# A projection kernel with context tokens: weights of the modulation in fours, context products merged, bias loads on another queue

## The chip, the cores and the metric

The kernel runs on one core of a Trainium2 chip. The metric is the device time of one execution in microseconds; a time stands for the median of several executions. TensorE (PE in the profile, with its weight loads as PEld) multiplies matrices, VectorE (DVE) and ScalarE (ACT) work element by element, GpSimd (POOL) does a little of that and issues DMAs, SyncE (SP) only issues DMAs. Each engine runs its own instructions in order, and waits for others through semaphores.

## The reference

One layer: an adaLN-modulated input goes through one wide projection; half of its columns feed a gated position-mixing MLP, the other half a bidirectional state-space scan; both come back through one output projection and a layer norm. Context tokens go through a part of the projection only. What the change touches is the beginning of it:

```python
D_MODEL, SEQ, CTX_LEN = 2048, 1024, 256; W_A = W_B = 1024
mod_x = jax.nn.silu(c) @ w_ada + b_ada                  # (1, 6144)
mod_c = (jax.nn.silu(c_ctx) @ w_ada + b_ada)[None]
shift_x, scale_x, gate_x = jnp.split(mod_x, 3, axis=-1)
shift_c, scale_c, gate_c = jnp.split(mod_c, 3, axis=-1)
proj_x = _modulate(x, shift_x, scale_x) @ w_in          # (1024, 5 * 1024)
hc = _modulate(ctx, shift_c, scale_c)                   # LN(ctx) * (1 + scale) + shift
ub_c = hc @ w_in[:, col_b0:col_b1]                      # (256, 1024)
...
mixed = einsum("hpq,bnqhd->bnphd", w_s, LN(v) * ln_g + ln_b) + b_s   # position mixing
ya_x = u * mixed * silu(za_x)
```

Everything is fp32.

## The kernel before

**Arithmetic.** Each operand of a main product is split in two: `hi` is the value rounded to the short fp32r format (ScalarE, `whi` for weights), `lo` what is left (VectorE, `wlo`). A product then is three: hi·hi, hi·lo, lo·hi (`kstep`, L825 to L829), all summed in one PSUM bank. Every instruction on an engine but the DMAs goes through one wrapper, so the trace gives all of them line L519, and they are told apart by the names of their tiles.

**Weights.** `w_in` comes in chunks of 128x1024 (512 KB), two to a block of 128 output columns: chunk c of a block holds the rows k = 8c to 8c+7 (of 16) of 128 each. `Weights` (L554 to L583) loads a chunk on SP's queue (`wraw`, every third one of the context pass `craw`, L565) and splits it; `wget` (L658) takes chunk i, issues the load of i+2 and then the split of i+1. `wraw`, `whi` and `wlo` have two buffers each, so a load waits for the split of an earlier chunk, and a split for TensorE to be done with an earlier one. Chunks 0 to 7 belong to the blocks v0 to v3, 8 and 9 to `zb` 0, 10 to 25 to the eight context blocks `cx` (chunk 11 is the second half of the first one).

**Prologue (L735 to L954).** `x` is normalised, transposed and modulated in 32 units (k, h) (k: 128 of the 2048 input columns; h: half of the rows), and each unit at once goes through three main products blocks (`pro_main`, b = 0, 1, 2). The shift and scale that unit k needs come from `matvec` (L767): `w_ada` comes in 64 segments `ada` of 512 KB, eight for each group s of 256 columns of `x`; a segment i is two fp32 products, into the quarters `q = i % 2 * 2 + j` (j = 0, 1) of the 128 output partitions of a `sy` bank. After the eighth, ScalarE copies the bank to `mvs` and `mods` (L784) sums its quarters by transposes and a VectorE reduction into `ss`. The loads: 16 segments lie in slots, 3 in `wpool`, the rest in a ring of five; when segment n is done, the load of n+5 is issued (`ada_load`, L748). The main loop runs over the 32 units; four steps (j = 0 to 3) belong to one group s = 2 to 7, and `cut` says which segments are taken after which step: `cut = 0, 3, 5, 7`, that is three after j = 0, two after j = 1, two after j = 2, and the last at the beginning of the step j = 3.

**Context pass (L1003 to L1103).** `ctx_task` makes the context tile `cT` (128 x 16 x 2 x 256: 16 k, hi and lo, 256 tokens), interleaved with the blocks v3 and zb0. Then `zb_out` evicts zb0 through SiLU (`szb`) and stores it on ScalarE's queue (`tmp_sz`). `bias_task` (L1043) loads `ws` and `bs` (512 KB each, in pieces of 512 B) on SP's queue, multiplies ones by `ws` (two `sy` products) and adds to `bs` on VectorE; its `bs` takes the buffer of `szb` (tag `stb`), so the load waits for that store. The loop over eight blocks m and 16 k makes three products of 256 columns for each k into `e[:, :256]`; ScalarE copies the block to `usc`, GpSimd's queue stores it (`tmp_ubc`):

```python
kstep([(e[:, :256], cxT)], wt, 8 * c + kk, c + kk == 0, c == 1 and kk == 7)
```

The interleaving of the tasks is decided while the program is built, by modelled clocks (`until`, `room`, `pump`), not on the chip.

Of the kernel before, what the change touches and what calls it, by code (L numbers as in the profile page):

```python
# [9 lines left out]
FT = mybir.dt.float32  # L10
FR = mybir.dt.float32r
I32 = mybir.dt.int32
AF = mybir.ActivationFunctionType
# [11 lines left out]
def dap(t, offset, ap):  # L25
    return bass.AP(tensor=t.tensor, offset=t.offset + offset, ap=[list(a) for a in ap])
# [559 lines left out]
def build(tc, a, out, scratch):  # L586
    nc = Metered(tc.nc)
    ck = nc.clock
    V, S, T, P, SP = nc.vector, nc.scalar, nc.tensor, nc.gpsimd, nc.sync
# [13 lines left out]
    def bank(tag, bufs):  # L603
        return (sb[1] if tag == "sb" else pp).tile([128, 512], FT, name=tag, tag=tag, bufs=bufs)

    def slot(dt, name, h):

        return slots.tile([128, 1024], dt, name=name, tag=f"slot{h}", bufs=16)

    def parts(name, h):  # L610
        t = slot(FR, name, h)
        return t[:, 0:512], t[:, 512:1024]


    chunks, first = [], {}
# [23 lines left out]
    W = Weights(nc, wpool, chunks)  # L639
# [18 lines left out]
    def wget(key, held=0):  # L658

        i = first[key]  # L660
        r = W.get(i)
        W.load_to(i + 2 - held)
        if not held:
            W.split_to(i + 1)
        return r
# [4 lines left out]
    def pump(n=1):  # L670
        for _ in range(n):
            for t in list(tasks):
                if next(t, StopIteration) is StopIteration:
                    tasks.remove(t)

    def wait(n):
        for _ in range(n):
            yield

    def until(t):  # L680

        while ck.pe < t:
            yield
# [11 lines left out]
    def drain(*ts):  # L695

        while any(t in tasks for t in ts) if ts else tasks:
            ck.pe += 1300
            pump()
# [13 lines left out]
    sc = consts.tile([128, 2, 16], FT, name="sc")  # L713
# [22 lines left out]
    pro_p = pro.enter_context(tc.tile_pool(name="pro", bufs=1))  # L736
# [4 lines left out]
    ada = {j: slot(FT, "ada", j // 8).rearrange("p (j c) -> p j c", j=2) for j in range(16)}  # L741
    xn = [[slot(FT, "xn", h).rearrange("p (t c) -> p t c", t=4) for h in range(2)] for _ in range(8)]

    def x_in(h, s0, s1):
        for s in range(s0, s1):
            SP.dma_start(xn[s][h], dap(a["x"], h * 512 * D + s * 256, [[D, 128], [128 * D, 4], [1, 256]]))

    def ada_load(j):  # L748
        if j < 64:
            if 15 < j < 19:  # L750
                ada[j] = wpool.tile([128, 2, 512], FT, name="ada", tag=("whi", "wlo", "wlo")[j - 16])
            elif j > 18:
                ada[j] = pro_p.tile([128, 2, 512], FT, name="ada", bufs=5)
            SP.dma_start(ada[j], a["w_mod"][j // 8, j // 2 % 4][:, j % 2 * 2:j % 2 * 2 + 2])

    def norm(s, h, ts=range(4)):
# [8 lines left out]
    mvb = {}  # L765

    def matvec(s, i0, i1):  # L767

        for i in range(i0, i1):
            if i == 0:  # L770
                mvb[s] = bank("sy", 1)
            n = 8 * s + i
            t = ada.pop(n)
            for j in range(2):
                q = i % 2 * 2 + j
                T.matmul(mvb[s][32 * q:32 * q + 32], cs[:, 2 * i + j], t[:, j], start=(i < 2), stop=(i > 5),
                         skip_group_check=True)
            if n > 18:
                ada_load(n + 5)
            if i == 7:  # L780
                mvs = mvb[s, 1] = pro_p.tile([128, 512], FT, name="mvs")
                S.activation(mvs, mvb[s], AF.Copy)

    def mods(s):  # L784
# [30 lines left out]
    def modulate(n):  # L815

        k, h = units[n]
        sh, sl = ss[:, k // 2, k % 2, 0:1], ss[:, k // 2, 2 + k % 2, 0:1]
        xm = pro_p.tile([128, 512], FT, name="xm")
        S.activation(xm, tp.pop(n), AF.Identity, bias=sh, scale=sl)  # L820
        hi, lo = xT[h][k] = parts("xT", h)
        S.activation(hi, xm, AF.Copy)
        V.tensor_sub(lo, xm, hi.bitcast(FT))

    def kstep(banks, wt, k, st, en):  # L825
        for p_, (i, j) in enumerate(((0, 0), (0, 1), (1, 0))):
            for o, x in banks:
                T.matmul(o, wt[i], x[k][j], start=st and p_ == 0, stop=en and p_ == 2,
                         skip_group_check=True)  # L829

    def block(key, order=(0, 1)):
        o = [bank("mm", 4) for _ in range(2)]
        n = 0
        for c in order:
            hi, lo = wget((key, c))
            for kk in range(8):
                k = 8 * c + kk
                wt = (hi[:, kk * 128:kk * 128 + 128], lo[:, kk * 128:kk * 128 + 128])
                kstep(list(zip(o, xT)), wt, k, n == 0, n == 15)
                n += 1  # L840
                pump()
        return o
# [5 lines left out]
    def pro_main(k, h, b):  # L848
# [3 lines left out]
        hi, lo = wt0[b, c]  # L852
        wt = (hi[:, kk * 128:kk * 128 + 128], lo[:, kk * 128:kk * 128 + 128])
        kstep([(vb[b][h], xT[h])], wt, k, k == 0, k == 15)
    cut = 0, 3, 5, 7
    units = [(k, h) for h in range(2) for k in range(2)] + [(k, h) for k in range(2, 16) for h in range(2)]

    def early(s):
# [19 lines left out]
    x_stats(0, 0, 8)  # L878
    ln_finish(0, 4)
    x_in(1, 0, 8)  # L880
    for j in range(8, 24):
        ada_load(j)
    w3_load(1)
    for s in range(8):
# [11 lines left out]
    for i, (k, h) in enumerate(units):  # L896
        s, j = divmod(i + 5, 4)
# [61 lines left out]
    def v_out(m, o):  # L959
        vg = st_p.tile([128, 1024], FT, name="vg", tag="sta")  # L960
        for h in range(2):
            S.activation(vg[:, halves[h]], o[h], AF.Gelu)
        vt = st_p.tile([128, 8, 128], FT, name="vt", tag="stb")
        yield from wait(2)
        for h in range(2):
            pt = bank(("ps", "sy")[h], 1)
            for i in range(4):
                T.transpose(pt[:, i * 128:i * 128 + 128], vg[:, (4 * h + i) * 128:(4 * h + i) * 128 + 128], ident)
            yield
            S.activation(vt[:, 4 * h:4 * h + 4].rearrange("p a b -> p (a b)"), pt, AF.Copy)  # L970
            for i in range(4):
                V.bn_stats(stats[:, 4 * h + i, m], vt[:, 4 * h + i])
            yield
        S.dma_start(scratch["v"][m], vt)

    def v_first():
        for b in (0, 2, 1):
            yield from v_out(b, vb[b])
        while len(vb) < 4:
            yield  # L980
        yield from v_out(3, vb[3])
    vf = v_first()
    next(vf)
    tasks.append(vf)

    def zb_out(m, o):
        zs = st_p.tile([128, 1024], FT, name="szb", tag="stb")
        for c in range(2):
            S.activation(zs[:, halves[c]], o[c], AF.Silu)
        S.dma_start(scratch["sz"][m], zs)  # L990
# [4 lines left out]
    cT = cT_p.tile([128, 16, 2, 256], FR, name="cT")  # L995
    cxT = {k: (cT[:, k, 0], cT[:, k, 1]) for k in range(16)}
# [38 lines left out]
    vb.append(o)  # L1035
    o = block(("zb", 0))
    drain()
    zb_out(0, o)

    cl_es.close()  # L1040
# [2 lines left out]
    def bias_task():  # L1043

        ws = st_p.tile([128, 8, 128], FT, name="ws", tag="sta")
        SP.dma_start(ws, dap(a["w_sp"], 0, [[128, 128], [16384, 8], [1, 128]]))
        bs = st_p.tile([128, 8, 128], FT, name="bs", tag="stb")
        SP.dma_start(bs, dap(a["b_sp"], 0, [[0, 128], [128, 8], [1, 128]]))
        yield from until(ck.pe + 20000)
        for h0 in (0, 4):  # L1050
            rs = bank("sy", 1)
            T.matmul(rs, ones, ws[:, h0:h0 + 4].rearrange("p h d -> p (h d)"), start=True, stop=True)
            yield from wait(2)
            for h in range(h0, h0 + 4):
                V.scalar_tensor_tensor(bs[:, h], rs[:, 128 * (h - h0):128 * (h - h0) + 128], vecs[:, 1, h:h + 1],
                                       bs[:, h], op0=OP.mult, op1=OP.add)
            yield from until(ck.pe + 4000)
        S.dma_start(dap(scratch["bp"], 0, [[128, 128], [16384, 8], [1, 128]]), bs)
# [34 lines left out]
    for m in range(8):  # L1093
        e = bank("sb", 2)
        for c in range(2):
            hi, lo = wget((("cx", m), c))
            for kk in range(8):
                wt = (hi[:, kk * 128:kk * 128 + 128], lo[:, kk * 128:kk * 128 + 128])
                kstep([(e[:, :256], cxT)], wt, 8 * c + kk, c + kk == 0, c == 1 and kk == 7)
                pump()  # L1100
        us = us_p.tile([128, 8, KC], FT, name="usc")
        S.activation(us[:, ::-1].rearrange("p j k -> p k j"), e[:, :256].rearrange("p (k j) -> p k j", j=8), AF.Copy)
        P.dma_start(dap(scratch["ubc"], m * 128 * 8 * KC, [[8 * KC, 128], [1, 8 * KC]]), us.rearrange("p j k -> p (j k)"))  # L1103
    drain()
    us_es.close()
# [126 lines left out]
    for m in range(8):  # L1232
        o = block(("ub", m))
        us = s2.tile([128, 8, KL], FT, name="us", tag="vh")
# [114 lines left out]
    for m in range(8):  # L1349
# [8 lines left out]
        for k in range(8):  # L1358
            wt = (hi[:, k * 128:k * 128 + 128], lo[:, k * 128:k * 128 + 128])
# [147 lines left out]
    for t in range(4, 8):  # L1507
# [7 lines left out]
        for i, x, y in ((0, 0, 1024), (1, 0, 1024)) if t < 7 else ((0, 0, 1024), (1, 0, 512), (1, 512, 1024)):  # L1515
            z, c = z1[t - 4, i][:, x:y], slice(1024 * i + x, 1024 * i + y)
# [60 lines left out]
```

## Times and profile before

| | us |
|---|---|
| median of 3 runs | 1620.19 |
| lowest, highest | 1620.13, 1622.97 |
| profiled execution | 1618.88 |
| its span (first to last instruction) | 1616.8 |
| PE busy | 1571.3 |
| DVE busy | 1071.4 |
| ACT busy | 504.5 |

The profile's times count from the start of the span of that one execution. An engine's busy time says how much of the span it worked, not whether the end waited for it; that is read from the chain of waits, which follows the work that ended last back from one releaser to the one before, and from the idle time that a row of the timeline shows in brackets ahead of an instruction, with what ended it. Beside them, PEclk is the TensorE clock that was granted, as a share of full speed (1.00 is 2.4 GHz, 0.50 is 1.2 GHz).

### The profile page before, as it was taken

The numbers are of one execution on the slowest core, as the hardware profiler recorded it, in microseconds if no ns is written. First come the engines' busy times: TensorE is split into PE (matmuls) and PEld (weight loads), VectorE is DVE, ScalarE is ACT, GpSimd is POOL, SyncE is SP. The second block draws the span as 40 slices with busy tenths as digits, with TensorE's granted clock in tenths as the row PEclk, the third lists the DMA queues.
The fourth block names the chain that finished last, engine by engine and source line by source line (L and its number), as shares of the span: only waits on it lengthen the run. The fifth ranks groups of instructions, "written<-read, shape, count | busy, mean of one in ns | idle before, by whom it ended". The sixth has DMA issues, their size and how long they took to land.

```text
span 1616.8 us, 22311 instructions
## 1 busy us (share of the span) xinstructions
PE 1571.3 (97%) x8468; PEld 1269.8 (79%) x8468; DVE 1071.4 (66%) x1960; ACT 504.5 (31%) x831; POOL 184.7 (11%) x286
## 2 busy tenths in 40 slices
PE   4999999999999999999999999999999999999996
PEld 2556889888888888888888888888888888888775
DVE  8542635982988889888888898166565633465557
ACT  2544653112322233233233333211533412133210
POOL 0000000000222222222222222121000000012000
PEclk9999999999999999999999999999999999999998
DMA  9885354334444444444434443477445533365422
GB/s 338 318 321 177 149 170 158 120 123 130 114 120 127 114 128 122 116 128 128 127 99 128 128 116 89 139 249 248 182 146 167 202 132 121 108 239 176 137 85 104
DMA packets 134211, 251.37 MB, mean 155 GB/s; under 512 B 53972, under 2 KB 74580, under 8 KB 132312
## 3 DMA queue, kind: packets, MB, share of 16 engines
q1 hardware_dynamic: 112200, 208.73, 39.9%
q0 software_dynamic: 16384, 31.78, 7.0%
q10 hardware_dynamic: 5520, 9.44, 1.6%
q8 instruction: 66, 1.08, 0.3%
q14 instruction: 41, 0.34, 0.1%
HBM read 213.60 MB, written 36.12 MB: 154 GB/s over the span
## 4 chain that ended last, share of the span: by engine, by line
PE 86%; DVE 5%; DMA 5%; ACT 3%; issue 1%; SPq 1%; ACTq 0%; DVEq 0%
PE mm L519 65%; PE sb L519 9%; PE sy L519 8%; PE ps L519 3%; DMA wraw<-in_w_out_dram 2%; DVE wlo L519 1%; ACT whi L519 1%; DVE stats L519 1%; DVE z L519 1%; DMA wraw<-in_w_in_dram 1%; DVE xn L519 1%; ACT xm L519 1%; DMA xn<-in_x_dram 1%; DMA cl<-in_ctx_dram 0%; DMA ada<-in_w_mod_dram 0%
## 5 line engine op out<-in xcount | busy, mean ns | idle before, releaser
L519 PE MATMUL mm<-xT,whi 128*128 128x512 f32 x2496 | 687.9, 395 | 1.6 <-ACT vg L519 0.7
L519 PEld LDWEIGHTS mm<-xT,whi 128*128 128x128 f32 x2496 | 462.0, 188 | 108.0 <-issue 6.9
L519 PE MATMUL mm<-xT,wlo 128*128 128x512 f32 x1248 | 391.4, 391 | 0.0
L519 DVE TENSOR_TENSOR wlo<-wraw,whi 128x1024 fp32r<-128x1024 f32 (+1 forms) x164 | 200.0, 1222 | 287.3 <-ACT whi L519 287.1
L519 ACT ACTIVATE whi<-wraw 128x1024 fp32r<-128x1024 f32 (+1 forms) x164 | 170.0, 1039 | 407.4 <-PE mm L519 212.5
L519 PEld LDWEIGHTS mm<-xT,wlo 128*128 128x128 f32 x1248 | 234.7, 188 | 50.8 <-DVE wlo L519 0.9
L519 DVE TENSOR_TENSOR p<-sb,ue 128x640 f32<-128x640 f32 x64 | 49.7, 819 | 50.0 <-PE sb L519 49.9
L519 PE MATMUL mm<-whi,yb 128*128 128x512 f32 x256 | 79.9, 389 | 0.0
L519 PE MATMUL mm<-y,whi 128*128 128x512 f32 x256 | 68.4, 389 | 0.0
L519 POOL TENSOR_TENSOR zs<-zs,dsk 128x16 f32<-128x16 f32 x32 | 18.1, 565 | 423.0 <-ACT zs L519 423.0
L519 PE MATMUL sy<-ada,cs 128*32 128x512 f32 x256 | 41.5, 621 | 18.8 <-DMA ada<-in_w_mod_dram 18.8
L519 PE MATMUL mm<-whi,ya 128*128 128x512 f32 x192 | 59.5, 389 | 0.0
L519 POOL TENSOR_TENSOR z<-z,lnb 128x1024 f32<-128x1024 f32 x8 | 19.2, 2396 | 346.0 <-ACT z L519 346.0
L519 PEld LDWEIGHTS mm<-whi,yb 128*128 128x128 f32 x256 | 48.1, 188 | 9.9
L519 PEld LDWEIGHTS mm<-y,whi 128*128 128x128 f32 x256 | 48.0, 188 | 9.9
L519 DVE TENSOR_TENSOR xT<-xm,xT 128x512 fp32r<-128x512 f32 x32 | 22.1, 692 | 49.5 <-ACT xT L519 49.5
L519 PE MATMUL sb<-cT,whi 128*128 128x256 f32 x256 | 48.6, 292 | 2.6 <-ACT whi L519 2.6
L519 PE MATMUL mm<-wlo,yb 128*128 128x512 f32 x128 | 49.9, 390 | 0.0
L519 DVE TENSOR_TENSOR_SCAN p<-ur,p 128x640 f32<-128x640 f32 x32 | 47.7, 1491 | 3.0 <-DVE ut L519 0.5
L519 PE MATMUL sb<-whi,yb 128*128 128x512 f32 x128 | 45.4, 396 | 1.5 <-ACT whi L519 1.5
L403 POOL DMA_DIRECT2D tmp_z<-zs x64 | 44.1, 691 | 11.2 <-POOL zs L519 9.2
L519 DVE TENSOR_TENSOR p<-p,ue 128x512 f32<-128x512 f32 x64 | 44.2, 690 | 1.7
(270 smaller groups left out, 2325.6 us busy)
## 6 DMA issues: line engine op xcount, KB each, us to landing
wraw<-in_w_in_dram SPq DMA_DIRECT2D x89, 512.0 KB
ada<-in_w_mod_dram SPq DMA_DIRECT2D x64, 512.0 KB
wraw<-in_w_out_dram SPq DMA_DIRECT2D x64, 512.0 KB
gw<-in_w_gate_dram POOLq DMA_DIRECT2D x32, 512.0 KB, 6.0
xn<-in_x_dram SPq DMA_DIRECT2D x16, 512.0 KB
upf<-tmp_pf SPq DMA_DIRECT2D x32, 256.0 KB
ubb<-in_b_c_dram SPq DMA_DIRECT2D x32, 256.0 KB
tmp_v<-vt ACTq DMA_DIRECT2D x8, 512.0 KB
```

What stands on the lines that cost most here:

```text
L403: nc.gpsimd.dma_start(dap(d["z5"], (z["g0"] + q) * 32 * 144, [[72, 2], [144, 32], [1, 72]]), zs[64 * q:64 * q + 64])
L519: r = f(*args, **kw)
```

## The change

There are five edits. (1) `cut` becomes `0, 4, 4, 8`: four segments after j = 0, none after j = 1, four after j = 2, none at j = 3; the ring of segments gets a sixth buffer, one more is loaded ahead, and `mvs` and `xm` take one buffer in turn. (2) The split of chunk 11 is issued ahead of the SiLU evictions of zb0. (3) A SiLU on one element, at the end of `v_first`, brings the function table load earlier. (4) `ws` and `bs` are loaded on GpSimd's queue. (5) In the context loop whi·[hi | lo] is one product of 512 columns into the whole bank `e`, and wlo·hi one of 256 into its first half; at the block's end VectorE adds the second half to `usc`.

```diff
-                ada[j] = pro_p.tile([128, 2, 512], FT, name="ada", bufs=5)
+                ada[j] = pro_p.tile([128, 2, 512], FT, name="ada", bufs=6)
...
-                ada_load(n + 5)
+                ada_load(n + 6)
             if i == 7:
-                mvs = mvb[s, 1] = pro_p.tile([128, 512], FT, name="mvs")
+                mvs = mvb[s, 1] = pro_p.tile([128, 512], FT, name="mvs", tag="mvs")
...
-        xm = pro_p.tile([128, 512], FT, name="xm")
+        xm = pro_p.tile([128, 512], FT, name="xm", tag="mvs")
...
-    cut = 0, 3, 5, 7
+    cut = 0, 4, 4, 8
...
-    for j in range(8, 24):
+    for j in range(8, 25):
         ada_load(j)
...
         yield from v_out(3, vb[3])
+        S.activation(sc[:, 1, 0:1], sc[:, 1, 0:1], AF.Silu)
...
     o = block(("zb", 0))
     drain()
+    W.split_to(first[("cx", 0), 1])
     zb_out(0, o)
...
-        SP.dma_start(ws, dap(a["w_sp"], 0, [[128, 128], [16384, 8], [1, 128]]))
+        P.dma_start(ws, dap(a["w_sp"], 0, [[128, 128], [16384, 8], [1, 128]]))
...
-        SP.dma_start(bs, dap(a["b_sp"], 0, [[0, 128], [128, 8], [1, 128]]))
+        P.dma_start(bs, dap(a["b_sp"], 0, [[0, 128], [128, 8], [1, 128]]))
...
-                kstep([(e[:, :256], cxT)], wt, 8 * c + kk, c + kk == 0, c == 1 and kk == 7)
+                k = 8 * c + kk
+                T.matmul(e, wt[0], cT[:, k].rearrange("p i t -> p (i t)"), start=k == 0, stop=False,
+                         skip_group_check=True)
+                T.matmul(e[:, :256], wt[1], cxT[k][0], start=False, stop=k == 15, skip_group_check=True)
                 pump()
...
-        S.activation(us[:, ::-1].rearrange("p j k -> p k j"), e[:, :256].rearrange("p (k j) -> p k j", j=8), AF.Copy)
+        usk = us[:, ::-1].rearrange("p j k -> p k j")
+        S.activation(usk, e[:, :256].rearrange("p (k j) -> p k j", j=8), AF.Copy)
+        V.tensor_add(usk, usk, e[:, 256:].rearrange("p (k j) -> p k j", j=8))
```

In the main loop of the prologue, TensorE's order before, from the end of a step j = 0 (the segments `sy<-ada,cs`; the products of the next unit; a transpose `ps<-io,xn`); a row counts each product once, the trace counts an fp32 one twice:

```order
L519 MATMUL sy<-ada,cs 32x512 x6
L519 MATMUL mm<-xT,whi 128x512 x2
L519 MATMUL mm<-xT,wlo 128x512
L519 MATMUL mm<-xT,whi 128x512 x2
L519 MATMUL mm<-xT,wlo 128x512
L519 MATMUL sb<-xT,whi 128x512 x2
L519 MATMUL sb<-xT,wlo 128x512
L519 MATMUL sy<-ada,cs 32x512 x4
L519 MATMUL ps<-io,xn 128x128 x4
```

The same place after:

```order
L519 MATMUL sy<-ada,cs 32x512 x8
L519 MATMUL mm<-xT,whi 128x512 x2
L519 MATMUL mm<-xT,wlo 128x512
L519 MATMUL mm<-xT,whi 128x512 x2
L519 MATMUL mm<-xT,wlo 128x512
L519 MATMUL sb<-xT,whi 128x512 x2
L519 MATMUL sb<-xT,wlo 128x512
L519 MATMUL ps<-io,xn 128x128 x4
```

The fourth segment joined the first three, and none is left between this step and the transpose of the next.

ScalarE's order before, from the last context tile to the eviction of the first context block:

```order
L519 ACTIVATE xm<-sb,ss 128x128
L519 ACTIVATE cT<-xm 128x128
L519 ACT_TABLE_LOAD
L519 ACTIVATE szb<-mm 128x512 x2
L990 DMA tmp_sz<-szb 128x1024
L519 ACTIVATE whi<-wraw 128x1024 x2
L519 ACTIVATE usc<-sb 128x32x8
```

The same place after:

```order
L519 ACTIVATE xm<-sb,ss 128x128
L519 ACTIVATE cT<-xm 128x128
L519 ACTIVATE whi<-wraw 128x1024
L519 ACTIVATE szb<-mm 128x512 x2
L991 DMA tmp_sz<-szb 128x1024
L519 ACTIVATE whi<-wraw 128x1024
L519 ACTIVATE usc<-sb 128x32x8
```

The first of the two `whi` (chunk 11) went ahead of the `szb` evictions, and the table load is gone from here.

SP's queue before, from the loads of chunks 11 and 12 on:

```order
L565 DMA wraw<-in_w_in_dram 128x1024 x2
L1046 DMA ws<-in_w_sp_dram 128x8x128
L1048 DMA bs<-in_b_sp_dram 128x1024
L565 DMA wraw<-in_w_in_dram 128x1024
L565 DMA craw<-in_w_in_dram 128x1024
L565 DMA wraw<-in_w_in_dram 128x1024 x2
```

The same place after:

```order
L565 DMA wraw<-in_w_in_dram 128x1024 x3
L565 DMA craw<-in_w_in_dram 128x1024
L565 DMA wraw<-in_w_in_dram 128x1024 x2
L565 DMA craw<-in_w_in_dram 128x1024
L565 DMA wraw<-in_w_in_dram 128x1024 x2
```

The load of chunk 13 now follows that of chunk 12 directly; `ws` and `bs` stand on GpSimd's queue ahead of the eight `tmp_ubc` stores.

## Rows read from the trace of the kernel before

**Rows 1.** Page, busy time: engine, us (share of the span), instructions.
```profile
PE 1571.3 (97%) x8468; PEld 1269.8 (79%) x8468; DVE 1071.4 (66%) x1960; ACT 504.5 (31%) x831; POOL 184.7 (11%) x286
```

**Rows 2.** Windows: us, busy PE PEld DVE ACT POOL, PEclk, DMA share, GB/s.
```profile
220.00:240.00 20.00, 19.48 (x149) 19.24 (x148) 6.64 (x7) 7.86 (x9) 1.82 (x3) 0.91 0.69 234
...
300.00:320.00 20.00, 20.00 (x90) 16.57 (x89) 19.15 (x49) 2.93 (x3) 0.53 (x1) 1.00 0.26 101
```

**Rows 3.** Chain of waits in the prologue: start us, us, what.
```profile
50.00 1.85 PE sy L519 x16
...
59.87 1.84 PE sy L519 x12
...
64.01 1.00 PE sy L519 x8
...
92.37 6.58 DMA ada<-in_w_mod_dram
```

**Rows 4.** Timeline of TensorE behind that transfer: start us, us, instruction [idle before].
```profile
98.99 1.05 PE L519 MATMUL sy<-ada,cs 128*32 128x512 f32 x4 [0.23 <-DMA ada<-in_w_mod_dram]
```

**Rows 5.** Window of 4 us in the prologue.
```profile
88.00:92.00 4.00, 4.00 (x22) 1.92 (x21) 2.12 (x5) 2.35 (x5) 0.00 (x0) 1.00 1.03 408
```

**Rows 6.** Timelines of ScalarE, VectorE, TensorE and SP, start of the context pass.
```profile
199.08 1.06 ACT L519 ACTIVATE whi<-wraw 128x1024 fp32r<-128x1024 f32 x1 [1.72 <-PE mm L519]
...
213.79 1.28 ACT L519 ACT_TABLE_LOAD   x1
...
216.58 2.00 ACT L519 ACTIVATE whi<-wraw 128x1024 fp32r<-128x1024 f32 x2 [0.40 <-ACT szb L519]
...
217.66 2.36 DVE L519 TENSOR_TENSOR wlo<-wraw,whi 128x1024 fp32r<-128x1024 f32 x2 [3.56 <-ACT whi L519]
...
212.10 0.40 PE L519 MATMUL sb<-cT,whi 128*128 128x256 f32 x2
...
217.68 0.50 PE L519 MATMUL sb<-cT,whi 128*128 128x256 f32 x2 [2.55 <-ACT whi L519]
...
226.98 0.39 PE L519 MATMUL sb<-cT,wlo 128*128 128x256 f32 x1 [0.52 <-DVE wlo L519]
...
218.88 0.33 SPq L1048 DMA_DIRECT2D bs<-in_b_sp_dram  x1
```

**Rows 7.** Chain of waits, in the context pass and further on.
```profile
219.31 5.22 DMA wraw<-in_w_in_dram
...
239.93 0.86 PE sy L519 x2
...
246.68 19.40 PE sb L519 x162
...
1378.30 43.52 PE mm L519 x192
...
1529.78 3.20 DMA wraw<-in_w_out_dram
```

**Rows 8.** Window of 1 us in the first context block.
```profile
221.00:222.00 1.00, 1.00 (x7) 1.00 (x7) 0.00 (x0) 0.00 (x0) 0.00 (x0) 0.50 0.80 201
```

**Rows 9.** Timelines of VectorE and of the weight loads, end of a context block.
```profile
231.45 1.23 DVE L519 TENSOR_TENSOR wlo<-wraw,whi 128x1024 fp32r<-128x1024 f32 x1 [2.99 <-ACT whi L519]
...
232.73 0.19 PEld L519 LDWEIGHTS sb<-cT,wlo 128*128 128x128 f32 x1
```

**Rows 10.** Timeline of VectorE; page, DMA queues (packets, MB, share) and issues.
```profile
240.83 1.13 DVE L519 SCALAR_TENSOR_TENSOR bs<-sy,vecs,bs 128x128 f32<-128x128 f32 x4
243.79 1.23 DVE L519 TENSOR_TENSOR wlo<-wraw,whi 128x1024 fp32r<-128x1024 f32 x1 [1.83 <-ACT whi L519]
...
288.40 0.43 DVE L519 TENSOR_TENSOR t<-pr,pi 128x256 f32<-128x256 f32 x1
...
q0 software_dynamic: 16384, 31.78, 7.0%
...
gw<-in_w_gate_dram POOLq DMA_DIRECT2D x32, 512.0 KB, 6.0
```

## The prediction, made before the changed kernel had run

> **What bounds the kernel now.** I read the busy table first: TensorE is busy 97% of the span, every other engine far less [rows 1]. So an edit pays only if it takes columns or passes from TensorE, or removes a wait of TensorE. The windows of 20 us say where that can be: at 300 to 320 TensorE is busy 20.00 of 20.00 us, while 220 to 240 shows 19.48 and a granted clock of 0.91 [rows 2]. Then the chain of waits of the two stages that the diff touches: in the prologue it runs through TensorE nearly all the time, with pieces `PE sy` (the w_ada products) between the main products, and one transfer of an `ada` segment [rows 3]; in the context pass it is products, one `wraw` transfer and one weight split [rows 7]. Last, the timelines of the engines around those waits [rows 4, 6, 9]. Behind the context pass the order of the instructions on every engine is the one of before, so nothing but a shift is to be expected there.
>
> **Prologue: segments in fours.** A segment is two fp32 products into 32 output partitions each; an even and an odd segment fill the four quarters of the partitions. The trace counts each such product twice, so x4 is one segment. The chain shows 1.85 us for x16 (four segments), 1.84 us for x12 (three), 1.00 us for x8 (two) [rows 3]: three cost as much as four. I read it so: products of different quarters run side by side, and a pass of one pair, full or half full, costs about 0.92 to 1.00 us. A group of eight was taken as 3, 2, then 2 and 1 back to back, that is 1.84 + 1.00 + 1.84 = 4.68 us, five passes. As 4 and 4 it is 2 x 1.85 = 3.70 us, four passes. 0.98 us less, for the six groups s = 2 to 7: **-5.9 us**. The number of products is unchanged, only their company.
>
> Is it all on the path? TensorE hardly waits in that stretch; the one wait that I find for a segment there is 0.23 us [rows 4]. Against the gain stands the supply: four segments are now wanted at once. A step takes 64.01 - 59.87 = 4.14 us with 1.84 us of segments in it [rows 3], so two steps and a group of four take 2 x 2.30 + 1.85 = 6.45 us, 4 x 0.524 MB in 6.45 us = 325 GB/s. The DMA engines have moved 408 GB/s over 4 us here [rows 5], at their limit (share 1.03). A load is released by the segment six before it, so the loads that a group's first half frees are wanted some 6.5 us later by the next group's second half, and a landing on the chain took 6.58 us [rows 3], with others queued ahead of it; the two are the first of their burst. The sixth buffer is what lets a load start one segment earlier. I cost the supply at nothing, and keep 0.1 us a group of four (12 of them, -1.2) for the low end; at the high end the 0.23 us wait and a little of the copy of `mvs` behind a weight split go too: 4.7 to 6.4. The tag that `mvs` and `xm` now share costs nothing: `xm` needs the sums made from `mvs` anyway.
>
> **Context pass: one product for both parts.** 256 columns go at 19.40/162 = 0.1198 us each, 512 columns at 43.52/192 = 0.2267 us [rows 7]. Per k it was 3 x 0.1198 = 0.3593, and becomes 0.2267 + 0.1198 = 0.3465: 0.0128 us x 128 = **-1.65 us**. Bounds: nothing (if the split of the next weights sets the pace), to 1.65.
>
> The Trainium skill ("TensorE: Matmul & The Clock Gate", section "Wait — 56ns, not 53.3ns?") gives a product N columns at 2.4 GHz plus about 2.5 ns. By it the merging would save 2.5 ns x 128 = 0.3 us (an estimate), the total coming out at 1610.1. The rows disagree: 119.8 - 106.7 = 13 ns at 256 columns and 226.7 - 213.3 = 13 ns at 512, and the rows decide.
>
> The added VectorE sum of each block is 128x256, 0.43 us by the row of that size [rows 10]. It runs beside the next ScalarE split, in the 2.99 us that VectorE waits before its `wlo` [rows 9]: nothing. If it stood in the way it would cost up to 8 x 0.43 = 3.4 us.
>
> **Context pass: the start.** The pass runs from 212.10 to 246.68 + 19.40 = 266.08, 53.98 us [rows 6, 7]. Products: 8 x 16 x 3 x 0.1198 = 46.0; two bias products at 239.93 [rows 7], twice 0.86 = 1.7; so 6.3 us are overhead. Seen of it: 2.55 us waiting for `whi` of chunk 11, the `wlo` behind it (its lo product could not start before 217.66 + 1.18 = 218.84, about 0.7), 0.52 us for the `wlo` of chunk 13 [rows 6], and a clock of 0.91 over 20 us, that is 1.8 us [rows 2]; in 221 to 222 the granted clock is 0.50, the lower level of 1.2 GHz, after the engine had stood still twice just before [rows 8]. The table load of 1.28 us and two SiLU evictions stand ahead of that `whi` on ScalarE [rows 6].
>
> Now the `whi` of chunk 11 stands ahead of the evictions: it begins at 213.79 where the table load did, ends about 214.85, `wlo` (1.23 [rows 9]) about 216.1. The first half of block 0 ends at about 215.0 (8 x 0.3465 from 212.10, and what the last context tiles cost). So the hi product of the next half starts at once, and only the lo product waits, from 215.2 to 216.1: 0.95 us in place of 3.3. With that short a pause I take it that the clock stays. The moved table load fits: ScalarE stands idle for 1.72 us before 199.08 [rows 6] against 1.28; at worst 1.28.
>
> Next in line is chunk 13. Its load (SP) waits for the `wlo` of chunk 11 to free a buffer, and before also stood behind the `bs` load, issued at 218.88 [rows 6], so it went at 219.31 and took 5.22 us [rows 7]. Now SP's queue holds no `ws` and `bs`, and it goes at 216.15. Landing takes 3.2 to 5.2 us [rows 7], then `whi` and `wlo`, 2.3: ready between 221.7 and 223.7, taken 222.7. Wanted: chunk 11 done 215.0 + 2.77 + 0.95 = 218.7, chunk 12 2.77 later, and one hi product: 221.75. So a **wait of 0 to 1.95, taken 0.95**, at the place of the 0.52 of before. Last, at each block's end the `wlo` ends 0.05 us before its weight load, 231.45 + 1.23 = 232.68 against 232.73 [rows 9]. With halves 0.10 us shorter that margin is gone: 0.05 x 8 = 0.4 lost. New overhead 0.95 + 0.95 + 0.4 + 0.1 (restarts) = 2.4. The pass: 6.3 - 2.4 + 1.65 = **-5.5 us**; ends 2.7 (clock falls again 1.8, chunk 13 at its worst 1.0) to 6.9 (chunk 13 in time, no margin lost).
>
> **Bias loads on GpSimd's queue.** What the move brings is SP's place in line (219.31 to 216.15), and only together with the earlier split: before, the `wlo` that frees the buffer ended at 218.84, just ahead of the `bs` issue at 218.88, so by itself it is worth at most 0.4 us. On GpSimd's queue `bs`, which waits for the `szb` store (issue about 218.6, hardly earlier), stands ahead of the `tmp_ubc` stores; nobody reads these in the pass. The Trainium skill ("DMA: Bandwidth & Descriptors", section "Issuing engines are not separate DMA queues") says that loads started by different engines run on the same 16 DMA engines and save only issue time. By that rule the move alone brings nothing, the total is 0.4 us higher at most, and the load of chunk 13 shares the engines with the `szb` store and `bs` wherever they are issued.
>
> **Sum.** -5.9 - 5.5 = -11.4. The profiled execution took 1618.88 us, so 1607.5; the median of the runs, 1620.19, stands 1.3 above it: **1608.8 us**. Its own range: gains of 7.4 to 13.3, 1606.9 to 1612.8.
>
> **Rivals.** A measurement tells about 0.2% (3.2 us) from no change, so faster means below 1617.0.
> 1. *The clock falls again* at the shorter pause, and chunk 13 is late: the pass gives 2.7. For: it did fall at this place [rows 8]. Against: the pause is a third. 5.9 + 2.7: 1611.6. Chance 0.12.
> 2. *The segments starve TensorE*, since 6.5 us is about the 6.58 us of a landing. At 0.3 us a group of four, 12 x 0.3 = 3.6: 1612.4. Against: 325 of 408 GB/s, and one wait of 0.23 in the stretch of before. Chance 0.10.
> 3. *Merging gives next to nothing*, the pace being set per column or by the splits: 1608.8 + 1.65 = 1610.5. Against: the two pitches [rows 7]. Chance 0.04. The rule of the Trainium skill on product pitch, above, would give 1610.1.
> 4. *`bs` lands late on GpSimd's queue.* VectorE's bias sum (now about 236.2, 240.83 before [rows 10]) waits for it with every later `wlo` behind it on VectorE, and TensorE stalls one for one, once the sum is more than 1.8 us late (VectorE then waited 1.83 before the next `wlo`, at 243.79 [rows 10]). This queue's loads of 512 KB land in 6.0 us, but in packets of 31.78 MB/16384 = 1.9 KB; `bs` comes in pieces of 512 B, four times as many [rows 10]. At 4 x 6.0 = 24 us it lands at 242.6, 4.6 us beyond 238: 1613.4, chance 0.03. **Slower than before** from 34 us on (218.6 + 34 = 252.6, 14.6 beyond 238, which eats 11.4 and 0.2%); at 37 us 1626. Chance 0.03: nothing in rows of this queue comes near.
> 5. *The gain is swallowed* late, by the w_out loads on the chain (`wraw` at 1529.78 [rows 7]): 1619 to 1620. Against: these loads wait for buffers that TensorE frees, in the same order, so they shift along. Chance 0.01.
>
> **How the numbers follow.** The forecast has the other 0.67. Of its and the first rivals' mass (0.96 with the late `bs` at 24 us) I take 0.02 for two of them at once, ending within 0.2%: faster 0.94, within 0.2% 0.02 + 0.01 = 0.03, slower 0.03. The range of 8 in 10 takes the forecast with its bounds and the first three rivals, and a microsecond for the median's own place over the profile: 1606.0 to 1613.5.
>
> **What would show it.** Right: `PE sy` pieces of the prologue all x16 at 1.85 and none x8, no wait on `ada`; the prologue 5.9 us shorter; `sb` products alternating 512 and 256 columns at 0.227 and 0.120; one pause near 1 us at about 209.3 (215.2 less 5.9), the granted clock 1.00 behind it, a second pause below 2 us at chunk 13; the pass 48.5 us long; everything behind it earlier by 11.4 us. Wrong: x16 pieces well above 1.85; the clock at 0.50 in a window of the pass; `bs` or `wlo` named before long waits of TensorE; pauses behind 266 that before did not have.

## The result

The changed kernel took 1612.53 us (median of 4 runs, 1610.12 to 1615.11) beside 1620.16 for the kernel before: a ratio of 0.9950, with a 95% interval of 0.9938 to 0.9962. It is 7.6 us faster, in the range that was forecast (1606.0 to 1613.5) and 3.7 us above the forecast of 1608.8. Measured again beside other kernels it took 1611.79, ratio 0.9938 (0.9926 to 0.9951). The time lies where the second rival had put it (1612.4: segments that starve TensorE). The experiments below show that this did happen, and that the context pass, too, gave about 1 us less than was forecast.

The busy table and two windows of the profile after, to hold beside [rows 1, 2] (the profiled execution took 1615.11, the slowest of the four; its span is 1613.3):

```profile
PE 1567.1 (97%) x8340; PEld 1260.7 (78%) x8340; DVE 1077.7 (67%) x1968; ACT 504.3 (31%) x832; POOL 185.5 (11%) x288
```
```profile
200.00:220.00 20.00, 19.27 (x103) 16.10 (x102) 8.72 (x20) 14.61 (x37) 0.57 (x1) 1.00 0.34 113
220.00:240.00 20.00, 19.13 (x104) 15.73 (x104) 11.28 (x14) 8.76 (x10) 2.18 (x4) 1.00 0.69 244
```

TensorE is still the bound, and it has 128 products fewer. In the context pass the granted clock is 1.00 in both windows, where 220 to 240 had 0.91.

**The prologue after.** The chain of waits there, to hold beside [rows 3] (start us, us, what):

```profile
62.16 1.85 PE sy L519 x16
...
84.05 7.78 DMA ada<-in_w_mod_dram
...
91.87 1.05 PE sy L519 x4
...
97.75 2.23 PE sy L519 x16
```

And three rows of TensorE's timeline, where [rows 4] had one:

```profile
89.60 1.91 PE L519 MATMUL sy<-ada,cs 128*32 128x512 f32 x12
91.87 1.05 PE L519 MATMUL sy<-ada,cs 128*32 128x512 f32 x4 [0.36 <-DMA ada<-in_w_mod_dram]
...
119.50 3.11 PE L519 MATMUL sy<-ada,cs 128*32 128x512 f32 x16
```

The first group of four takes 1.85 us, as forecast. The one at 89.60 does not: three segments are there; the fourth lands 7.78 us after its issue, keeps TensorE waiting for 0.36 us behind the three, and then runs alone, 1.05 us. So a late segment costs twice: the wait, and a pass that it should have shared. At 97.75 and 119.50 waits hide inside a piece: 2.23 and 3.11 us for the work of 1.85. Rows of idle time thus show only a part of it (0.5 us in this stretch); the length of the pieces shows it. One more wait is new: behind the group at 105.13, a product waits 0.34 us for a `wlo`, and this group of eight takes 14.37 us where a whole one takes 13.75. The kernel before has no wait there; every run below that takes the segments in fours or in pairs has it.

**The context pass after**, timelines of ScalarE, VectorE and TensorE, to hold beside [rows 6]:

```profile
213.18 1.04 ACT L519 ACTIVATE whi<-wraw 128x1024 fp32r<-128x1024 f32 x1
214.13 1.06 ACT L519 ACTIVATE szb<-mm 128x512 f32<-128x512 f32 x2
...
214.25 1.23 DVE L519 TENSOR_TENSOR wlo<-wraw,whi 128x1024 fp32r<-128x1024 f32 x1 [0.65 <-PE sb L519]
...
215.53 0.39 PE L519 MATMUL sb<-cT,wlo 128*128 128x256 f32 x1 [0.73 <-DVE wlo L519]
...
222.51 0.38 PE L519 MATMUL sb<-cT,wlo 128*128 128x256 f32 x1 [0.76 <-DVE wlo L519]
```

and the chain of waits there, beside [rows 7]:

```profile
215.51 4.54 DMA wraw<-in_w_in_dram
...
242.04 19.19 PE sb L519 x108
261.23 3.88 PE mm L519 x17
```

The split of chunk 11 stands ahead of the evictions, the table load is gone, the pause is 0.73 us in place of 2.55 and, just behind, 0.76. Chunk 13 is late: issued at 215.51, landed at 220.05, split by 222.46. The pass runs from 211.60 to 261.23: 49.6 us, 4.35 less than before.

### The profile page after: what moved, and what is told of

Read it like the earlier page. It is cut to its first block, busy times and chain, and to the rows that moved or that the text cites. A ratio compares the mean times of both kernels' runs of the same rounds, so it can differ in the third digit from the quotient of the medians.

```text
span 1613.3 us, 22086 instructions
## 1 busy us (share of the span) xinstructions
PE 1567.1 (97%) x8340; PEld 1260.7 (78%) x8340; DVE 1077.7 (67%) x1968; ACT 504.3 (31%) x832; POOL 185.5 (11%) x288
## 4 chain that ended last, share of the span: by engine, by line
PE 84%; DMA 6%; DVE 5%; ACT 2%; SPq 1%; issue 1%; ACTq 0%; DVEq 0%
PE mm L519 64%; PE sb L519 9%; PE sy L519 8%; PE ps L519 3%; DMA wraw<-in_w_out_dram 2%; DVE wlo L519 2%; DMA ada<-in_w_mod_dram 1%; ACT whi L519 1%; DVE z L519 1%; DVE stats L519 1%; DVE xn L519 1%; DMA xn<-in_x_dram 1%; DMA wraw<-in_w_in_dram 1%; DMA ubb<-in_b_c_dram 0%; DMA cl<-in_ctx_dram 0%
## 5 line engine op out<-in xcount | busy, mean ns | idle before, releaser
L519 PE MATMUL mm<-whi,ya 128*128 128x512 f32 x192 | 59.6, 389 | 0.0
L519 PE MATMUL mm<-wlo,yb 128*128 128x512 f32 x128 | 49.9, 390 | 0.4 <-DVE wlo L519 0.4
L519 PE MATMUL sb<-cT,whi 128*128 128x512 f32 x128 | 46.2, 401 | 0.1
```

What stands on the lines that cost most here:

```text
L519: r = f(*args, **kw)
```

## The experiments

Two stretches are read from every profile: P, from the first segment of s = 2 to the transposes of `mvs` of s = 7, and C, the context pass from its first product to the first product behind it (before: P 59.80 to 146.10, C 212.10 to 266.08). They are free of what happened ahead of them, but each value comes from one profiled execution: in the six profiles that take the segments as before, P spreads from 85.8 to 87.1.

| kernel | median us | ratio to before (95%) | P us | C us |
|---|---|---|---|---|
| before | 1620.2 to 1621.4 | 1 | 86.3 | 54.0 |
| changed kernel | 1612.53 | 0.9950 (0.9938 to 0.9962) | 83.5 | 49.6 |
| changed, again (e5) | 1611.79 | 0.9938 (0.9926 to 0.9951) | 81.9 | 49.4 |
| prologue alone (e1) | 1616.43 | 0.9974 (0.9964 to 0.9984) | 81.9 | 54.0 |
| context alone (e2) | 1615.55 | 0.9970 (0.9959 to 0.9981) | 87.0 | 49.5 |
| segments in pairs (e3) | 1609.94 | 0.9938 (0.9925 to 0.9950) | 82.3 | 49.4 |
| half the bytes (e4) | 1607.52 | 0.9921 (0.9907 to 0.9934) | 79.4 | 49.4 |
| ring of five (e6) | 1614.79 | 0.9958 (0.9944 to 0.9971) | 84.6 | 49.4 |
| eviction behind the split (e7) | 1609.58 | 0.9922 (0.9910 to 0.9935) | 83.9 | 47.3 |
| pairs and eviction (e8) | 1608.02 | 0.9915 (0.9902 to 0.9929) | 81.7 | 47.3 |
| merged product alone (e9) | 1620.39 | 0.9998 (0.9989 to 1.0007) | 87.1 | 53.7 |
| start of the pass alone (e10) | 1616.84 | 0.9975 (0.9965 to 0.9985) | 86.4 | 49.9 |
| bias loads alone (e11) | 1619.49 | 0.9993 (0.9984 to 1.0002) | 86.3 | 53.2 |
| shared buffer alone (e12) | 1619.98 (one run) | | 85.8 | 54.1 |

### Which part brought what: the prologue's edits alone, the context's alone

```diff
 # e1: the kernel before with
-    cut = 0, 3, 5, 7
+    cut = 0, 4, 4, 8
...
 # and the ring of six, ada_load(n + 6), 25 loads ahead, one tag for mvs and xm; e2: all the other edits
```

> The kernel before with the prologue edits alone (segments taken 4 and 4, ring of six, one tag for mvs and xm). Forecast's theory: 5.9 us faster than before, about 1614.3. Theory S (starvation: a group of four asks for four loads at once, the late segment makes TensorE wait and then costs a pass of its own; the trace of after shows about 4.7 us of this over s = 4 to 7): 1 to 3 us faster, 1617 to 1619. Theory C (the segments are in time in most executions; what is missing in the profiled execution of after is a fall of the clock near 50 us, by chance): 5 to 6 us faster in the median, and any execution without that fall shows it in full.

> The kernel before with the context pass's edits alone. By the prediction 5.5 us faster, about 1614.7; by the trace of after, where the pass takes 49.6 us in place of 54.0, 4.4 us faster, about 1615.8, with the sum of the two parts making up the whole 7.6. If the parts disturb each other, the two single gains add up to more or less than 7.6 by over 2 us.

The prologue alone brought 4.0 us of the median (1616.43 beside 1620.4), the context pass 4.9; their sum, 8.8, is the whole within what a measurement tells (7.6, and 9.6 at e5), so the parts don't disturb each other. The context is near its forecast of 5.5; the prologue falls short of 5.9 by about two. It lies between what theories S and C said of it; P is shorter by 4.4 us in the profile.

### Is it the supply of segments: half the bytes, pairs, a shorter ring

```diff
 # e4: ring segments (j > 18) loaded to half
-            SP.dma_start(ada[j], a["w_mod"][j // 8, j // 2 % 4][:, j % 2 * 2:j % 2 * 2 + 2])
+                SP.dma_start(ada[j][:, 0], a["w_mod"][j // 8, j // 2 % 4][:, j % 2 * 2])
...
 # e3
-    cut = 0, 4, 4, 8
+    cut = 0, 2, 4, 6
...
 # e6: bufs=5, ada_load(n + 5), 24 loads ahead, with cut = 0, 4, 4, 8
```

> The changed kernel with each ring segment loaded to half only (256 KB; the second product of a segment reads the first half, so half of w_ada is left out of the shift and scale of groups s = 2 to 7): the same instructions on TensorE, half the traffic. Theory S in both forms: no wait on segments, 3.5 to 4.7 us faster than the changed kernel, 1608 to 1609. Theory C: no difference in the median, 1612 to 1613.

With half the bytes, every group of four in TensorE's timeline is a whole one:

```profile
87.68 1.92 PE L519 MATMUL sy<-ada,cs 128*32 128x512 f32 x16
...
94.36 1.92 PE L519 MATMUL sy<-ada,cs 128*32 128x512 f32 x16
...
115.83 1.92 PE L519 MATMUL sy<-ada,cs 128*32 128x512 f32 x16
```

P falls to 79.4 us, 6.9 below before, with the same instructions on TensorE. The forecast's 5.9 is thus there, and one more; what the supply takes is 4.1 us in the profiled execution of the changed kernel (83.5), 2.4 in those of e1 and e5 (81.9). The time is 1607.5, below the forecast.

> The changed kernel with the ring of segments at five buffers as before (loads n+5, one fewer loaded ahead), still 4 and 4. Theory S, latency form (a load has only the time from the release of its buffer to its use, and that must be longer than a landing): one buffer less takes a sixth of that time away, 3 to 6 us slower than the changed kernel, 1615 to 1618. Theory S, bandwidth form (the DMA engines can't move 305 GB/s beside the rest): the depth of the ring doesn't matter, within 1 us of the changed kernel. Theory C: the same, within 1 us.

The ring of five is 3.0 us slower than the changed kernel beside it (1614.79 and 1611.79; P 84.6 and 81.9), at the lower end of what the latency form said. The intervals of the two ratios still overlap a little (0.9944 to 0.9971, and 0.9926 to 0.9951), with five runs of each. A late segment in its timeline:

```profile
88.59 2.21 PE L519 MATMUL sy<-ada,cs 128*32 128x512 f32 x12
91.51 1.05 PE L519 MATMUL sy<-ada,cs 128*32 128x512 f32 x4 [0.71 <-DMA ada<-in_w_mod_dram]
```

So, as far as five runs of each can tell, the bytes alone don't decide: the same traffic with one buffer more is faster. What fits both this and e4 is the time from the release of a buffer to the use of what is loaded into it, against landings of up to 7.8 us (8.1 for the segment above); fewer bytes help if they land sooner, which was not read from e4.

> The changed kernel with the segments taken in pairs, two at each of the four steps (cut 0, 2, 4, 6): the same four passes for each eight segments, but loads are asked for two at a time. Theory S, burst form: the waits on segments go, about 4 us faster than the changed kernel, 1608 to 1609. Theory S, bandwidth form (the mean rate of about 305 GB/s is what the loads can't hold): no better than the changed kernel, 1612. Theory C: like the changed kernel, within 1 us. In each case up to 0.4 us a group may be lost since mvs is copied later.

Pairs at each step, with the same four passes, took 1609.94, about 2 us below the two medians of the changed kernel. But its ratio to the kernel before, 0.9938 (0.9925 to 0.9950), is that of the changed kernel at e5 (0.9926 to 0.9951), so a gain from pairs is not shown. Its profile still has late segments (P 82.3). The burst is a part of the loss at most.

> The changed kernel itself again, beside the kernels of this call. Theory S: a profiled execution again shows segments that come late (x16 pieces over 2 us, or pieces split by a wait on an ada transfer), some 2.5 to 4 us of it over s = 2 to 7, and the median again about 7.6 us below before, 1612 to 1613. Theory C: without a fall of the clock near 50 us it is within 1 us of 1609.

The second profile of the changed kernel shows late segments again:

```profile
96.97 2.42 PE L519 MATMUL sy<-ada,cs 128*32 128x512 f32 x16
...
121.25 1.05 PE L519 MATMUL sy<-ada,cs 128*32 128x512 f32 x4 [0.44 <-DMA ada<-in_w_mod_dram]
```

Another piece takes 2.31 us. By theory C the segments are in time in most executions; they are late in all four profiles of this prologue (the changed kernel, e5, e1, e7), so it falls. The median, 1611.79 and not 1609, doesn't refute it by itself, since this profile has the lower clock near 50 us too, and how many of the other runs had it is not known.

### What the context pass is made of

```diff
 # e9: before with the merged product and the VectorE sum only
+                T.matmul(e, wt[0], cT[:, k].rearrange("p i t -> p (i t)"), start=k == 0, stop=False,
...
 # e10: before with these only
+        S.activation(sc[:, 1, 0:1], sc[:, 1, 0:1], AF.Silu)
...
+    W.split_to(first[("cx", 0), 1])
...
+        P.dma_start(ws, dap(a["w_sp"], 0, [[128, 128], [16384, 8], [1, 128]]))
...
 # e11: the two P.dma_start only
```

> The kernel before with the early split of chunk 11, the early SiLU and the bias loads on GpSimd's queue, without the merged product. By the forecast 6.3 - 1.9 - 0.1 = 4.3 us less in the pass, about 1616; the clock at 1.00 throughout the pass. By the trace of after (waits of 0.73 and about 1.2 us are left) 3.9 us less. If the start depends on the merged product, less than 3.

> The kernel before with the merged context product and the added VectorE sum alone. Forecast: 1.65 us less columns, 0.4 lost at the block ends, 1.2 us faster, 1619.2 beside 1620.4. Theory D (the sum takes 0.65 us on VectorE ahead of the split and the pace of a block is set by it): the pass of 54.0 us shrinks by 0.4 to 0.8 only, no difference that can be measured. Rule of 2.5 ns a product: 0.3 less.

> The kernel before with the bias loads on GpSimd's queue alone. Forecast: the load of chunk 13 goes at 218.9 in place of 219.3, at most 0.4 us faster; the lower clock in 220 to 224 stays. If the queue's loads were slow for pieces of 512 B (24 us): bs lands at about 242, the bias sum 2 us late, slower by at most 0.5 us here.

The edits at the start bring C from 54.0 to 49.9 us, 4.1 of the 4.35, and 4.2 us of time. The merged product alone brings nothing that can be measured (0.9998), and in its profile 0.25 us of C; there the lower clock lasted longer, a window to hold beside [rows 2]:

```profile
220.00:240.00 20.00, 18.31 (x86) 15.22 (x87) 8.63 (x9) 8.09 (x10) 1.28 (x2) 0.83 0.67 226
```

That is not what took the 1.65 us: beside e10, where the clock is 1.00 throughout, the changed kernel too is only 0.25 us shorter (49.9 and 49.6). The chains of e10 and of e9, from the product on that waits for the split of chunk 13:

```profile
223.16 12.98 PE sb L519 x106
...
242.88 19.43 PE sb L519 x162
```
```profile
230.68 12.81 PE sb L519 x71
...
250.19 19.16 PE sb L519 x108
```

From there to the end of the pass, merging saves 0.43 us in either pair of kernels: 39.10 in before and 38.67 in e9, 39.15 in e10 and 38.72 in the changed kernel. For the 104 of 128 steps of k that lie there, 1.33 was worked out; some 0.9 are lost on the way, and e7 below shows where. Ahead of that place nothing is gained: in the changed kernel and e10 it hangs on the load of chunk 13, issued 3.91 us into the pass in both, and both merged kernels come to it 0.2 us later than their partners. The bias loads alone gave 0.75 us of C, where the wait of 0.52 at chunk 13 is gone; in the time this is no difference that can be measured.

```diff
 # e7: changed kernel with
+            hi, lo = wget((("cx", m), c))
+            if late:
+                evict(*late)
...
-        if i % 3 == 2 and first[("cx", 0), 0] + 3 < i <= first[("cx", 7), 1]:
+        if i % 3 == 1 and first[("cx", 0), 0] + 2 < i <= first[("cx", 7), 1]:
```

> The changed kernel with two things moved in the context pass: a block's eviction (ScalarE copy, VectorE sum, store) is issued after the next weight split and not ahead of it, and chunk 13 is loaded into the single craw buffer (chunks 13, 16, ... 25 in place of 14, 17, ... 23), so that its load waits for no split. The forecast costed the added sum at nothing and the lost margin at 0.4 us in all; the trace of after has the pass at 49.6 us against 46.1 of products. Theory D (the eviction ahead of the split, now 0.65 us copy and 0.65 us sum, sets the pace at each block's end): 1 us less in the pass; chunk 13 in time: another 1.2 us less; together 2 us faster than the changed kernel, about 1610.5. If the margin was all: 0.4 and 1.2 us. If what is slow is the product itself: only the 1.2 of chunk 13.

C is 47.3 us, 2.3 less than the changed kernel, as theory D had it. The end of a block in the changed kernel, timelines of ScalarE and VectorE, to hold beside [rows 9]:

```profile
225.37 0.65 ACT L519 ACTIVATE usc<-sb 128x256 f32<-128x256 f32 x1 [2.91 <-PE sb L519]
225.79 1.09 ACT L519 ACTIVATE whi<-wraw 128x1024 fp32r<-128x1024 f32 x1
...
226.05 0.66 DVE L519 TENSOR_TENSOR usc<-usc,sb 128x256 f32<-128x256 f32 x1 [2.33 <-ACT usc L519]
226.91 1.23 DVE L519 TENSOR_TENSOR wlo<-wraw,whi 128x1024 fp32r<-128x1024 f32 x1 [0.20 <-ACT whi L519]
```

The sum takes 0.66 us and not 0.43, but it is not what holds `wlo` up: VectorE waits another 0.20 us for `whi`. What sets the pace is ScalarE: it copies the finished block first and splits then, and the halves that cover this are now shorter. With the copy behind the split, the chain has, of the same 108 products,

```profile
214.78 18.08 PE sb L519 x103
...
239.43 18.73 PE sb L519 x108
```

18.73 us where the changed kernel took 19.19; 54 x 0.3465 = 18.71. So the merged product costs what the rows had said, and the copy ahead of the split took back 0.46 us at the three block ends of this stretch, 0.15 at each. At the six block ends behind chunk 13 that makes 0.9, which is what was missing above. The other 1.4 us of e7 are nearly all chunk 13, whose lo product came 1.3 us later in the changed kernel than the pitch of its neighbours would have it: no wait is left there (18.08 us in one piece).

### The shared buffer

```diff
-                mvs = mvb[s, 1] = pro_p.tile([128, 512], FT, name="mvs")
+                mvs = mvb[s, 1] = pro_p.tile([128, 512], FT, name="mvs", tag="mvs")
...
 # and the same tag for xm, in the kernel before
```

> The kernel before with mvs and xm in one buffer and nothing else. Forecast: costs nothing. Theory T (the copy to mvs must wait until VectorE has read the xm ahead of it): the transposes of mvs near 56 us wait some 0.4 us for ScalarE's copy, once; a time within 1 us of before.

TensorE and ScalarE in that kernel:

```profile
56.41 0.66 PE L519 MATMUL sy<-io,mvs 128*128 128x128 f32 x4 [0.39 <-ACT mvs L519]
...
55.76 0.60 ACT L519 ACTIVATE mvs<-sy 128x512 f32<-128x512 f32 x1 [0.82 <-DVE xT L519]
```

Theory T holds: the copy must wait until VectorE has read `xm`, and the transposes wait 0.39 us, once. The changed kernel has the same wait (0.38), the kernel before has none.

### A version that is faster than both

> The version to which the experiments point: the changed kernel with segments in pairs at each step, and the evictions and chunk 13 as in the other kernel of this call. Theory S and D: 2.5 (pairs) plus 2 us faster than the changed kernel, about 1608; the part of the waits that pairs leave (2.9 us in the profiled execution) stays.

1608.02 us, 0.9915 (0.9902 to 0.9929): 13.4 us below the median of before measured beside it, and 3.8 below that of the changed kernel. It joins e3 and e7. What the pairs add to e7 is not shown: 1608.02 and 1609.58, with ratios of 0.9915 and 0.9922 whose intervals overlap. P is 81.7, where six groups of the 14.0 us that its undisturbed ones take, less the 3.8 us that lie ahead of the first segment, would give some 80: one group has a late segment (a piece of 2.60 us in place of 1.92), and one the wait for the weight split. A ring of seven, which would test the reading of the ring of five from the other side, was not run; there is no room for it beside the other tiles of the prologue.

## Why the prediction was right, and where it was off

**Passes.** Right: four segments run in 1.85 us, and without late segments P shrinks by 6.9 us where 5.9 was worked out. A whole group of eight takes 13.75 us where it took 14.88, 1.13 less and not 0.98; five passes cost a little more than the pieces' sum. Six times 1.13 is 6.8; the kernel before also lost 0.8 us in two groups (15.16 and 15.36 us), which went too, and the new wait for a weight split took 0.65 back (14.40 in e4).

**Supply: the step that failed.** "I cost the supply at nothing." The working stood on a mean rate (325 of 408 GB/s) and on the two loads of a burst being first in line. The runs show 2.4 to 4.1 us lost in P, and the prediction's own sign of being wrong, x16 pieces well above 1.85 (2.23 and 3.11). The same paragraph had the number that decides: 6.5 us from release to use against a landing of 6.58; landings here reach 7.78. An allowance equal to a landing that has been seen is no allowance. The price was in the second rival, at 3.6 us, and it should have been the likeliest case. What was not seen at all is the second price of a late segment, the pass of its own, although [rows 4] shows it for the kernel before: the segment that came 0.23 us late ran alone, 1.05 us. That the time still fell into the range is in part luck: the passes gave one us more than was worked out, which paid for some of this.

**Shared tag: wrong, and small.** It was costed at nothing since `xm` needs the sums made from `mvs`; the other direction, the copy to `mvs` that waits for a reader of `xm`, was not looked at: 0.39 us.

**Start of the pass: right.** Pause 0.73 (0.95 forecast), clock 1.00 (granted in all windows of the pass), chunk 13 late by some 1.3 us (0.76 shown, the rest just ahead of it, at the late hi product; 0.95 taken, up to 1.95), its load issued 3.91 us into the pass (4.05 forecast), landing 4.54. The SiLU table load ahead fitted into the idle time.

**Merged product: right by itself, mis-sized at the block's end.** 13 ns a product are saved: with the evictions out of the way, e7 shows 18.73 us for 54 steps of k where the pitch behind the 1.65 gives 18.71. The Trainium skill's 2.5 ns a product ("TensorE: Matmul & The Clock Gate", section "Wait — 56ns, not 53.3ns?") would have given 0.3 us in all, an estimate; the trace of e7, with 13 ns, does not agree. The lost margin was put at 0.05 us a block, 0.4; it was 0.15, 0.9 in all. The VectorE sum cost nothing, as said, though it took 0.66 and not 0.43 us.

**Bias loads: right.** `bs` on GpSimd's queue was not late: it landed 4.6 us after its issue, the bias sum ran at 236.24 as worked out, and TensorE didn't wait for it, with pieces of 512 B. The slower rival had no part in it.

```profile
219.29 0.57 POOL L1050 DMA_DIRECT2D bs<-in_b_sp_dram  x1 [21.31 <-ACT usc L519]
...
236.24 1.13 DVE L519 SCALAR_TENSOR_TENSOR bs<-sy,vecs,bs 128x128 f32<-128x128 f32 x4
```

**"Nothing but a shift behind the pass": nearly.** In the profiled execution TensorE is only 0.5 us ahead at the start of the pass (2.8 gained in P, less 2.3 by which it came to P later, see the last section), 4.85 at the end of the pass, and 3.5 at the end of the span. Of the difference 1.0 is lost at 393, where a weight chunk behind the scan's small loads came late:

```profile
393.08 1.20 PE L519 MATMUL mm<-xT,whi 128*128 128x512 f32 x4 [0.34 <-ACT whi L519]
```

In other profiles the same place lost between nothing (e8) and 1.8 us (e3) with the same order of instructions, and the last 200 us gave back or took up to 1.4; no edit goes with it. It is part of the spread of 5 us between single runs of the changed kernel.

## What to carry to other kernels

Where small products share the array, count passes and not products: here three segments cost what four do (1.84 and 1.85 us), until a member comes late, and then it costs a pass of its own (1.05) besides the wait. Size a prefetch ring by the time from release to use against the longest landing seen, and not by mean bandwidth alone; where the two were equal here (6.5 us, and 6.58 seen before the change), there were waits, hidden inside pieces that should be shorter. When TensorE's half of a loop gets shorter, look again at everything on the other engines that stood between a block's end and its next operand: what is not needed at once (an eviction) goes behind what is.

## What the runs showed of the hardware that was not expected

The start of the prologue, up to about 57 us, is the same code in every kernel here but for the shared buffer, and for the loading of the segments, and yet its length differs by 3.8 us between profiles (the transposes of `mvs` near 56 us stand at 55.8 to 59.6; the shared buffer's wait is 0.4 of it). One place explains some 1.5 to 2 us. TensorE waits there for VectorE's statistics, at a time that VectorE sets, and a group of four follows; in the changed kernel, and with half the bytes:

```profile
47.83 0.66 PE L519 MATMUL mm<-io,xn 128*128 128x128 f32 x4 [1.18 <-ACT xn L519]
...
50.20 3.38 PE L519 MATMUL sy<-ada,cs 128*32 128x512 f32 x16
...
51.00:52.00 1.00, 1.00 (x12) 0.29 (x8) 0.17 (x1) 0.77 (x2) 0.00 (x0) 0.50 1.03 410
```
```profile
47.52 0.66 PE L519 MATMUL mm<-io,xn 128*128 128x128 f32 x4 [0.58 <-ACT xn L519]
...
49.74 1.92 PE L519 MATMUL sy<-ada,cs 128*32 128x512 f32 x16
...
51.00:52.00 1.00, 1.00 (x12) 0.41 (x5) 0.62 (x1) 0.35 (x1) 0.00 (x0) 1.00 0.99 397
```

In the five profiles where that pause was 0.90 to 1.18 us, the group behind it took 3.4 to 3.6 us (granted clock 0.50, 1.2 GHz, in the window shown); in the nine where it was 0.15 to 0.86, it took 1.92. The pause is longer where the clock had risen earlier on the way there and TensorE arrived sooner: the mean granted clock of 36 to 47 us is 0.76 to 0.84 in the five, 0.67 to 0.76 in the nine. TensorE gains some tenths, waits them off, and then loses 1.5 us to the lower clock. This goes together in fourteen profiles; no run changed the pause by itself, so that the pause is the cause is not shown. No kernel goes with it (e2 and e9, whose prologue is the one of before, have it; before and e10 have not), so a single profile of this kernel carries 1.5 us and more of chance from here.
